# Remainders of plain weight blocks by a negated copy on ScalarE and an accumulating DMA, in place of a subtraction on VectorE

## The chip, the cores and the metric

The kernel runs on one core of one Trainium2 chip, as one launch. The metric is the device time of that launch in microseconds (us), the median of three runs. Beside it stands one profiled execution, whose trace gives the start and the duration of every instruction on TensorE (PE, its weight loads PEld), VectorE (DVE), ScalarE (ACT) and GpSimd (POOL), and the issue and landing of every DMA. SyncE (SP) only issues DMAs here.

## The reference

One inference step of a one-layer trunk on 640 tokens (512 of a prompt, 8 x 16 of running streams), model width 1024. The combined projection `z = x @ w_in` has 6656 columns, which are split into the inputs of three branches; then comes the output projection and a SwiGLU block, each with a LayerNorm.

```python
z = x @ w_in
xa, ya, glu, q, gates = jnp.split(z, COL_SPLITS, axis=-1)
xa_c = causal_depthwise_conv(xa_hist, conv_a_w, conv_a_b)          # width 4
h, h_last = rg_lru(xa_c, h_prev, ...)                              # gates by block products, then a scan
out_a = (h * jax.nn.gelu(ya)) @ proj_a
u = glu[..., :D_CONV] * jax.nn.sigmoid(glu[..., D_CONV:])
v = causal_depthwise_conv(u_hist, conv_b_w, conv_b_b)              # width 31
out_b = jax.nn.silu(layer_norm(v, ln_b_g, ln_b_b)) @ proj_b
out_c = mem_cross_attention(q, mem_k, mem_v) @ proj_c
g = jax.nn.sigmoid(gates + b_gate)
merged = g[:, :, 0] * out_a + g[:, :, 1] * out_b + g[:, :, 2] * out_c
x = layer_norm(DEEPNORM_ALPHA * x + merged @ w_out, ln1_g, ln1_b)
ffn = (jax.nn.silu(x @ w_ffn_gate) * (x @ w_ffn_up)) @ w_ffn_down
x = layer_norm(DEEPNORM_ALPHA * x + ffn, ln2_g, ln2_b)
```

All inputs and outputs are float32.

## The kernel before, in words

**Three products for one.** Each float32 factor is held as two parts in the type fp32r, which TensorE multiplies fast: `hi`, the rounded value, and `lo`, the remainder. A product is `hi·hi + hi·lo + lo·hi`. The activations stand as `xh` and `xl`, a weight block as `wh` and `wl`. For a weight block the raw float32 values come from memory into a tile `wr`; ScalarE copies them with rounding into `wh` (`prep_hi`, the call of `copy`), and VectorE subtracts, `wl = wr - wh` (`prep_lo`).

**Steps and loads.** The program is a list of `Step`s, run in order. A plain block is a step made by `x_step`: 128 columns of a weight against the 640 tokens in two halves `c` of 320, over eight rows of 128, so 48 matmuls (`fm`), in the order `hi·xh`, `hi·xl`, `lo·xh` for each row: the remainder is first needed by the fifth and sixth matmul of a block. One `Load` of 1 MB brings two blocks; there are two `wr` tiles, and a new load is issued by SP (`pump`, line 253) when both blocks of a tile have been used up (`take`, called in `prep_lo`).

**When a block is prepared.** At step i the loop at the end of `trunk` first calls `prep_hi` for the block of step i+2; then it issues the first matmuls of step i, then the eviction of step i-1 (`flush`), then pieces of the side work (`advance`), then `prep_lo` of the block of step i+2. `wh` and `wl` have three buffers each, so the copy for step i+2 waits for the last matmul of step i-1. Results stand in PSUM in the tiles `pu`, four of them, two to a step: step i+1 needs the two that step i-1 used, when their eviction is done.

**Side work.** The convolutions, the attention, the recurrence (`lru`) and the LayerNorms are generators ("streams"). `advance` takes pieces from them as long as a reckoned time of VectorE and ScalarE, kept by `price_vector` and `price_scalar`, is behind that of TensorE. Each engine runs its own instructions in the order in which they were written down. POOL issues the loads of the attention caches (line 997), of the recurrence's weights (line 1163) and a few stores, and runs some small operations.

**The blocks by name**, in the order of the steps: the GLU gates 0 and 1 and the GLU input 0 (one group of three, whose matmuls are mixed), GLU input 1 ("GA1"), four blocks of the query ("Q0" to "Q3"), GLU gates 2, 3 and inputs 2, 3; eight recurrence inputs ("XA0" to "XA7"); eight gates of branch 2 ("C2_0" to "C2_7"), eight blocks of `proj_c`; then gates of branch 1 in pairs ("C1_0" and "C1_1", ...), each pair followed by two blocks of `proj_b` of half the length ("pb0", "pb1", ...); eight recurrence gates ("YA0" to "YA7"); then products by another scheme (`seven`), `proj_a`, `w_out`; the first four blocks of the feed-forward (gate 0, gate 1 and up 0 in a group of three, and up 1, "UP1"), and the rest by `seven` and by tokens.

`x_step` is called 48 times. Six of the calls belong to the two groups of three.

## Time and profile before

| | |
|---|---|
| median of 3 runs | 1047.9 us (1047.83 to 1047.99) |
| profiled execution | 1048.17 us, its span 1046.4 us |
| granted TensorE clock | 0.998 |
| TensorE busy | 1034.9 us |
| VectorE busy | 801.9 us |
| ScalarE busy | 499.2 us |
| GpSimd busy | 83.8 us |
| DMA | 128.89 MB; the queue of POOL's DMAs 28.23 MB |

A share of the whole span is a mean over many stages. The questions for this change are asked of single places: when a block's parts are ready, when the first matmul needs them, and what stands in the same queue.

### The profile page before, as it was taken

How to read it: one execution, taken by the hardware profiler on the slowest of the kernel's cores; microseconds unless marked ns; L12 is line 12 of the kernel's file. 1: busy time of each engine (PE TensorE's matmuls, PEld its weight loads, DVE VectorE, ACT ScalarE, POOL GpSimd, SP SyncE). 2: the span in 40 equal slices, each digit the busy share in tenths (PEclk: the TensorE clock that was granted, in tenths of full speed). 3: DMA queues.
4: the chain of work that ended last, by engine and by line, in shares of the span. 5: the costliest groups of instructions: out<-in, count | busy, mean ns of one | idle time of the engine just before them, and what ended most of it. 6: DMA issues, size and time to landing. Idle time of an engine off the chain costs nothing.

```text
span 1046.4 us, 16741 instructions
## 1 busy us (share of the span) xinstructions
PE 1034.9 (99%) x6689; PEld 984.0 (94%) x6689; DVE 801.9 (77%) x1412; ACT 499.2 (48%) x894; POOL 83.8 (8%) x152
## 2 busy tenths in 40 slices
PE   9999999999999999999999999999999999999997
PEld 5899999999999999999998899999999999888886
DVE  5769988899657855999595578888888887576875
ACT  5733655254576449566232455444444334444350
POOL 0000404200000000000211210000000001000111
PEclk9999999999999999999999999999999999999999
DMA  9722216531121221212636222222222223733581
GB/s 346 256 96 82 89 42 228 205 105 56 41 101 61 102 81 47 81 62 79 256 149 220 102 101 79 84 81 81 82 81 87 101 96 106 312 125 122 181 281 40
DMA packets 29854, 128.89 MB, mean 123 GB/s; under 512 B 4016, under 2 KB 4848, under 8 KB 19920
## 3 DMA queue, kind: packets, MB, share of 16 engines
q1 hardware_dynamic: 21168, 99.59, 26.9%
q0 software_dynamic: 8608, 28.23, 7.4%
q8 instruction: 52, 0.85, 0.3%
q14 instruction: 26, 0.21, 0.1%
HBM read 115.31 MB, written 12.50 MB: 122 GB/s over the span
## 4 chain that ended last, share of the span: by engine, by line
PE 92%; DVE 3%; ACT 2%; DMA 2%; issue 1%; SPq 0%; DVEq 0%; POOL 0%; ACTq 0%
PE pu L64 82%; PE pv L64 10%; DVE s L64 1%; ACT s L64 1%; DVE wl L64 1%; DMA s<-in_w_mem_v 1%; DMA s<-in_w_mem_k 0%; DMA s<-in_x_prompt 0%; DVE xres L64 0%; ACT wh L64 0%; ACT xh L64 0%; DVE wh L64 0%; DVE st L64 0%; DVE xl L64 0%; ACT L64 0%
## 5 line engine op out<-in xcount | busy, mean ns | idle before, releaser
L64 PE MATMUL pu<-xh,wh 128*128 128x320 f32 x1040 | 243.0, 310 | 1.1 <-DVE wh L64 0.6
L64 PE MATMUL pu<-xh,wl 128*128 128x320 f32 x1040 | 241.2, 309 | 0.0
L64 ACT ACTIVATE wh<-wr 128x1024 fp32r<-128x1024 f32 (+1 forms) x149 | 135.0, 908 | 214.2 <-PE pu L64 125.2
L64 PE MATMUL pu<-xl,wh 128*128 128x320 f32 x888 | 213.5, 309 | 0.0
L64 DVE TENSOR_TENSOR s<-s,s 128x640 f32<-128x640 f32 (+5 forms) x206 | 144.8, 722 | 52.6 <-ACT s L64 50.0
L64 PE MATMUL pu<-s,wh 128*128 128x320 f32 x1064 | 184.6, 309 | 0.0
L64 PEld LDWEIGHTS pu<-xh,wh 128*128 128x128 f32 x1040 | 175.2, 188 | 3.2 <-ACT xh L64 1.0
L64 PEld LDWEIGHTS pu<-xh,wl 128*128 128x128 f32 x1040 | 175.7, 188 | 0.0
L64 DVE TENSOR_TENSOR wl<-wr,wh 128x1024 fp32r<-128x1024 f32 (+1 forms) x113 | 129.2, 1145 | 56.4 <-ACT wh L64 56.3
L64 PEld LDWEIGHTS pu<-s,wh 128*128 128x128 f32 x1064 | 163.2, 188 | 0.3 <-DVE wh L64 0.3
L64 PEld LDWEIGHTS pu<-xl,wh 128*128 128x128 f32 x888 | 151.9, 188 | 0.0
L64 PE MATMUL pu<-s,wl 128*128 128x320 f32 x808 | 146.9, 309 | 0.5 <-DVE s L64 0.5
L64 DVE TENSOR_TENSOR s<-s,pu 128x320 f32<-128x320 f32 x188 | 88.6, 485 | 64.1 <-PE pu L64 60.7
L64 ACT ACTIVATE s<-s 128x640 fp32r<-128x640 f32 (+4 forms) x148 | 90.0, 627 | 87.4 <-DVE s L64 76.3
L64 PEld LDWEIGHTS pu<-s,wl 128*128 128x128 f32 x808 | 125.5, 188 | 0.9 <-issue 0.9
L64 DVE SCALAR_TENSOR_TENSOR s<-s,pb,s 128x511 f32<-128x511 f32 (+14 forms) x240 | 112.1, 539 | 2.9 <-ACT s L64 2.9
L64 PE MATMUL pu<-wh,s 128*128 128x512 f32 x364 | 107.1, 383 | 0.1
L64 PEld LDWEIGHTS pu<-wh,s 128*128 128x128 f32 x364 | 66.8, 188 | 14.2 <-ACT wh L64 1.2
L64 ACT ACTIVATE s<-pu 128x320 f32<-128x320 f32 (+2 forms) x90 | 36.5, 439 | 66.6 <-PE pu L64 66.4
L64 PE MATMUL pu<-s,s 128*128 128x512 f32 (+1 forms) x236 | 61.7, 411 | 0.5 <-DMA s<-in_w_mem_k 0.5
L64 PE MATMUL pu<-wl,s 128*128 128x512 f32 x182 | 57.1, 381 | 0.0
L64 PEld LDWEIGHTS pu<-s,s 128*128 128x128 f32 x236 | 42.6, 188 | 14.8 <-issue 5.5
(124 smaller groups left out, 1123.0 us busy)
## 6 DMA issues: line engine op xcount, KB each, us to landing
wr<-in_w_in SPq DMA_DIRECT2D x26, 1024.0 KB, 4.8
wr<-in_w_ffn_down SPq DMA_DIRECT2D x19, 1024.0 KB, 4.9
wr<-in_w_ffn_gate SPq DMA_DIRECT2D x11, 1024.0 KB, 4.7
wr<-in_w_ffn_up SPq DMA_DIRECT2D x11, 1024.0 KB, 4.8
s<-in_cache_k POOLq DMA_DIRECT2D x16, 256.0 KB, 5.2
s<-in_cache_v POOLq DMA_DIRECT2D x16, 256.0 KB, 5.1
wr<-in_proj_a SPq DMA_DIRECT2D x4, 1024.0 KB, 7.7
wr<-in_w_out SPq DMA_DIRECT2D x4, 1024.0 KB, 4.9
```

Source lines behind the costliest of these rows:

```text
L64: return f(*a, **k)
```

## The change

`Step` gets an argument `dram`. Where it is given, `prep_hi` lets ScalarE write the block twice: rounded into `wh`, and with scale -1 into `wl`. Then POOL issues a DMA that takes the block from memory once more (512 KB) and adds it to what stands in `wl`; the weight minus its rounded value is left. `prep_lo` no longer subtracts for such a block. It still calls `take`, so the load that follows waits for the readers of `wr` that are left, which are ScalarE's. `x_step` gives `dram` where `group` is None.

```diff
-                     half=None, after=None):
+                     half=None, after=None, dram=None):
+            self.dram = dram
...
-            for h, _, x in self.todo:
+            for h, l, x in self.todo:
                 copy(h, x)
+                if self.dram is not None:
+                    A.activation(l, x, AF.Copy, scale=-1.0)
+            if self.dram is not None:
+                h, l, x = self.todo[0]
+                G.dma_start(l, self.dram(self.ld.ap()), accum_op=OP.add)
             self.w = (hi, lo)
...
-            for h, l, x in self.todo:
+            for h, l, x in self.todo if self.dram is None else ():
                 self.eng.tensor_tensor(l, x, f32(h), op=OP.subtract)
             self.todo = None
             self.ld.take()
...
-        s = Step(ld, lambda r: r[:, o // 128], [128, KD, 128], mm, lambda: evac([x[:, :HT] for x in s.p]))
+        s = Step(ld, lambda r: r[:, o // 128], [128, KD, 128], mm, lambda: evac([x[:, :HT] for x in s.p]),
+                 dram=(lambda w: w[:, o // 128]) if group is None else None)
```

## The prediction

> **What bounds the kernel now.** I read the page first, then the table of windows, then the groups, then the timeline at single places.

> ```profile
> span 1046.4 us, 16741 instructions
> PE 1034.9 (99%) x6689; PEld 984.0 (94%) x6689; DVE 801.9 (77%) x1412; ACT 499.2 (48%) x894; POOL 83.8 (8%) x152
> ...
> PE 92%; DVE 3%; ACT 2%; DMA 2%; issue 1%; SPq 0%; DVEq 0%; POOL 0%; ACTq 0%
> ```

> TensorE is busy for 99% of the span and is 92% of the chain that ended last. The windows say how much it ever waits (columns: stretch, length, then busy time of PE, PEld, DVE, ACT, POOL):

> ```profile
> 49.00:1038.00 989.00, 987.57 (x6466) 949.04 (x6466) 764.62 (x1333) 465.73 (x833) 78.50 (x138) 1.00 0.32 114
> 49.00:454.00 405.00, 405.00 (x2930) 401.43 (x2930) 319.64 (x596) 219.93 (x412) 37.03 (x68) 1.00 0.26 92
> 454.00:456.00 2.00, 1.29 (x7) 0.76 (x6) 2.00 (x5) 0.96 (x2) 0.00 (x0) 1.00 0.00 0
> 649.00:651.00 2.00, 1.76 (x12) 1.52 (x11) 1.69 (x4) 0.00 (x0) 0.00 (x0) 1.00 0.00 0
> ```

> Between 49 and 1038 us it stands still for 989.00 - 987.57 = 1.43 us, half of that (0.71) at 454 to 456, where VectorE is busy throughout, and 0.24 at 649. So relief of VectorE can give back 1.43 us at the very most. What counts is whether a new wait reaches TensorE.

> **The change, part by part.**

> ```profile
> L64 DVE TENSOR_TENSOR wl<-wr,wh 128x1024 fp32r<-128x1024 f32 x97 | 118.2, 1221 | 46.3 <-ACT wh L64 46.3
> L64 ACT ACTIVATE wh<-wr 128x1024 fp32r<-128x1024 f32 x97 | 102.5, 1060 | 186.1 <-PE pu L64 97.2 <-issue 46.2 <-PE pv L64 23.8
> wr<-in_w_in SPq DMA_DIRECT2D x26, 1024.0 KB, 4.8
> wr<-in_proj_b SPq DMA_DIRECT2D x4, 512.0 KB, 3.2
> ```

> Of the 48 calls of x_step 42 are outside the groups, so by the code 42 blocks change, not 48. *Removed:* 42 subtractions of 1.22 us, 51 us of VectorE. It hides under TensorE nearly everywhere, so I count no gain except at the 0.71 us stop, where nothing removed lies near (the last removed one is in YA7); I credit 0.4 us, half of it. *Added on ScalarE:* 42 copies of the same shape as wh, 1.06 us each, 45 us on an engine with 499 busy. *Added on POOL:* 42 DMAs of 512 KB.

> *The landing of the new DMA* is the unknown; no accumulating DMA is in the trace. A plain 512 KB takes 3.2 us, which is the lower bound. An addition has to fetch the old contents too, so 1 MB passes the engines; a plain 1 MB takes 4.8. POOL's own loads are slower than SP's: 256 KB on a quiet stretch took 3.1, nearly what SP needs for twice that, so I add 0.5 and take **5.3 us** when nothing else moves. Beside a load these rows stand:

> ```profile
> L1163 POOL DMA_DIRECT2D s<-in_lru_w x1: 536/536/536, 298.7 to 298.7; - x1
> DMA to landing us min/median/max: 3.1/3.1/3.1
> L253 SPq DMA_DIRECT2D wr<-in_w_in x1: 328/328/328, 182.1 to 182.1; - x1
> DMA to landing us min/median/max: 8.3/8.3/8.3
> L997 POOL DMA_DIRECT2D s<-in_cache_v x4: 536/536/545, 182.6 to 184.3; - x4
> DMA to landing us min/median/max: 6.6/7.4/7.6
> ```

> Four loads of POOL, together 1 MB, beside one 1 MB load of SP landed after 6.6 to 7.6 us. An accumulate that moves 1 MB beside a load is that case; I take **7.6**. For the upper bound I let the addition cost 3 us more in both cases (8.3 and 10.6: the load's row above shows that crowding alone can take 8.3 instead of 4.8).

> *How long the DMA may take* is read at each block: the start of wh, plus 2 x 1.06 us for the two copies, plus 0.1 for the semaphore, against the first matmul that reads wl. Most blocks have 9 to 16 us, for two whole blocks (14 us) lie between. The short ones follow a group of three or two half-length pb steps:

> ```profile
> 51.98 1.06 ACT L64 ACTIVATE wh<-wr 128x1024 fp32r<-128x1024 f32 x1 [2.25 <-PE pu L64]
> 54.32 0.33 SPq L253 DMA_DIRECT2D wr<-in_w_in  x1
> 59.41 0.45 PE L64 MATMUL pu<-xh,wl 128*128 128x320 f32 x2
> 312.21 1.06 ACT L64 ACTIVATE wh<-wr 128x1024 fp32r<-128x1024 f32 x1 [0.52 <-PE pu L64]
> 319.93 0.46 PE L64 MATMUL pu<-xh,wl 128*128 128x320 f32 x2
> 354.45 1.06 ACT L64 ACTIVATE wh<-wr 128x1024 fp32r<-128x1024 f32 x1
> 363.05 0.46 PE L64 MATMUL pu<-xh,wl 128*128 128x320 f32 x2
> 626.27 1.06 ACT L64 ACTIVATE wh<-wr 128x1024 fp32r<-128x1024 f32 x1 [3.68 <-PE pu L64]
> 632.09 0.33 SPq L253 DMA_DIRECT2D wr<-in_w_ffn_up  x1
> 633.69 0.46 PE L64 MATMUL pu<-xh,wl 128*128 128x320 f32 x2
> ```

> - GA1: issue at 51.98 + 2.12 + 0.1 = 54.2, needed at 59.41: 5.2 us. It is the second block of its tile, so take lets SP issue the next 1 MB load as soon as the negated copy is done, at the same moment (in the rows it goes out at 54.32, after the subtraction). 7.6 - 5.2 = **2.4 us** of waiting.
> - UP1: issue at 628.5, needed at 633.69: 5.2 us, and again the next load (632.09 in the rows, after a late subtraction) moves up to 628.4. **2.4 us.**
> - C1_2: issue at 314.4, needed at 319.93: 5.5 us, first block of its tile, no load beside it: 5.3 lands 0.2 before. C1_4 is alike. C1_6: 356.7 to 363.05, 6.4 us. Nothing, but if the cover is gone each us late costs a us.

> *ScalarE's queue.* Behind the negated copy stands the eviction of the step before, on which PSUM of the step after depends. It is 1.06 us later. Where a softmax or a table load has already held ScalarE up, that is not free:

> ```profile
> 211.31 0.94 ACT L64 ACTIVATE s<-pu,pa 128x320 f32<-128x320 f32 x2
> 212.55 0.46 PE L64 MATMUL pu<-xh,wh 128*128 128x320 f32 x2
> 314.58 0.94 ACT L64 ACTIVATE s<-pu,pa 128x320 f32<-128x320 f32 x2
> 315.82 0.75 PE L64 MATMUL pu<-s,wh 128*128 128x320 f32 x4
> 409.55 0.77 ACT L64 ACTIVATE s<-pu 128x320 f32<-128x320 f32 x2
> 410.86 0.46 PE L64 MATMUL pu<-xh,wh 128*128 128x320 f32 x2
> ```

> The second half's matmul comes 0.15 after the first. At 212: eviction ends 212.25 + 1.06 = 213.31 against 212.70, 0.6 late. At 315: 316.58 against 315.97, 0.6. At 410: 411.38 against 411.01, 0.4. Together **1.6 us**. The dispatcher's reckoned time of ScalarE grows by the copy too, so side work moves elsewhere; bounds 0 and twice that (3.2).

> *POOL's queue.* The DMA waits for ScalarE, and everything behind it on POOL waits with it. Today POOL runs far ahead of the program:

> ```profile
> 175.06 2.70 POOL L997 DMA_DIRECT2D s<-in_cache_k  x5 [4.28 <-PE pv L64]
> 194.52 1.86 PE pv L64 x32
> 203.62 1.86 PE pv L64 x32
> ```

> The key loads of heads 2 and 3 stand in the program after the scores of heads 0 and 1 (194.52), yet were issued by 177.8. Now they stand behind C2_1's accumulate, which goes out at about 189.9; eight issues end at 194.2. With SP's load and the accumulate's double traffic 4 MB are under way from 189.4. Two MB side by side took 8.3 us in the rows above; two more at 3.2 each (4.8 against 3.2 us for half a MB more) make 14.7: landed at 204.1, head 2's half 3.2 earlier. Needed are head 2's keys at 203.62 and head 3's half of 1.86 us later, at 204.5. Zero, but with 0.4 us to spare. The recurrence's weights come later as well, and ScalarE's rounding of them waits in queue some 4 us; the step's eviction stands before it, so zero too. SP's queue gains: loads go out earlier, but had time.

> **Sum:** 2.4 + 2.4 + 1.6 - 0.4 = 6.0 us. From the profiled execution's 1048.17 this gives 1054.2; the median stood 0.27 lower, so **1053.9**.

> [...]

> **Rivals.**

> *The DMA is hidden anyway* (chance 0.29). It lands like a plain copy: 3.2 to 3.7 quiet, and beside a load no later than the 5.2 us that GA1 and UP1 have, or SP's load loses the race. Then only the evictions count, 0 to 1.6, less 0.4: 1047.5 to 1049.1. For it: the DMA share in the window row from 49 to 454 is 0.26. Against: the load leaves at the very same moment.

> *The addition is slow* (0.18). At 8.3 and 10.6 us: GA1 and UP1 5.4 each, C1_2 and C1_4 2.8 each, C1_6 1.9, the keys of head 3 up to 2.6 (3 less the 0.4), evictions 1.6, less 0.4: 22.1 us, 1070.0. Over 14 us even ordinary blocks would wait and it would be 42 times the excess; I give that 0.03 of the 0.18. Nothing in the trace speaks for or against a rate of adding.

> *Faster* (0.03). VectorE's relief decides at 454 and 649, where its queue is what TensorE waits for: all 1.43 us come back, 1046.5. It decides only if every new DMA lands inside 5.2 us and evictions keep their margins; even then it is inside 0.2%, so more than that needs the start as well, and no changed block is prepared before 52 us.

> **How the numbers follow.** A measurement of this kernel tells about 0.2% (2.1 us) from no change. My case, waits of 2.1 to 12 us, has 0.50; hidden 0.29; slow 0.18; faster 0.03. So faster 0.03, same 0.29, slower 0.68. The range takes in the hidden case from 1047.2 and the slow one to 1070. The likeliest case's own range is 1050 to 1060.

> **What would show it.** VectorE's wl rows 97 down to 55; 42 ACT rows that write wl and 42 POOL DMAs into wl, landing 5 to 8 us. TensorE's waits at 59.4 and 633.7 released by a DMA into wl, about 2.4 us each, in place of nothing; waits on ACT near 212, 315 and 410; none in Q, XA or most of C2. Wrong if the DMA lands under 5 us beside a load, if it takes over 8 alone, or if POOL's cache loads arrive late and TensorE stops at the scores near 204.

## The result, and the profile after

The changed kernel takes 1084.2 us (median of 4 runs, 1083.1 to 1084.7) against 1047.95; the ratio is 1.0343, with an interval of 1.0331 to 1.0355. The forecast was 1053.9 with a range up to 1070: slower, as predicted, but by 36.2 us where 6.0 were.

The page of the changed kernel:

```profile
span 1083.0 us, 16839 instructions
PE 1045.8 (97%) x6689; PEld 992.1 (92%) x6689; DVE 755.0 (70%) x1370; ACT 539.0 (50%) x937; POOL 119.2 (11%) x194
...
L298 POOL DMA_DIRECT2D wl<-in_w_in x41 | 36.3, 886 | 330.4 <-ACT wl L64 278.0
...
wl<-in_w_in POOLq DMA_DIRECT2D x41, 512.0 KB, 7.8
```

The work moved as the diff says. VectorE has 42 instructions and 46.9 us less, ScalarE 39.8 us more, and POOL issues 41 accumulates from `w_in` and one from `w_ffn_up`. TensorE has the same 6689 matmuls, but its busy time is 10.9 us longer (1045.8 against 1034.9). The rest of the loss is idle time. The windows (stretch, length, busy time of PE, PEld, DVE, ACT, POOL, then the granted clock, the DMA share and GB/s), and after them the list of what TensorE waited for (total, times, longest):

```profile
49.00:1075.00 1026.00, 998.62 (x6472) 956.73 (x6471) 718.05 (x1292) 505.36 (x876) 114.55 (x180) 0.99 0.44 131
```

```profile
PE pu L64 <- DMA wl<-in_w_in: 11.4, 4, 3.9
PE pv L64 <- ACT s L64: 8.7, 1, 8.7
PE pv L64 <- DVE s L64: 3.0, 1, 3.0
PE pu L64 <- DMA wl<-in_w_ffn_up: 2.5, 1, 2.5
```

TensorE now stands still for 1026.00 - 998.62 = 27.4 us, where it was 1.4. So 26.0 us are stops and 10.9 us longer busy time; together 36.9, and the span grew by 36.6. The first and the fourth row are accumulates that land late. The second is one single stop of 8.7 us.

Most of the longer busy time follows the stops. Three stops (60 us, 236 us, 321 us), each with the stretch behind it:

```profile
59.40:62.70 3.30, 0.02 (x1) 0.00 (x0) 0.43 (x2) 1.53 (x3) 0.88 (x1) 0.84 1.02 176
62.70:71.70 9.00, 8.97 (x43) 8.97 (x44) 0.00 (x0) 0.00 (x0) 0.00 (x0) 0.68 0.76 211
...
236.20:244.90 8.70, 0.02 (x3) 0.01 (x3) 1.31 (x2) 2.42 (x6) 4.07 (x8) 0.67 1.03 325
244.90:251.90 7.00, 7.00 (x84) 6.39 (x85) 4.55 (x10) 3.92 (x7) 0.00 (x0) 0.68 0.43 158
320.80:324.70 3.90, 0.04 (x2) 0.03 (x1) 3.74 (x6) 3.83 (x6) 0.03 (x1) 0.97 0.94 216
324.70:328.50 3.80, 3.80 (x16) 3.80 (x17) 0.00 (x0) 0.31 (x1) 0.00 (x0) 0.58 1.02 287
```

TensorE is busy throughout behind each stop, but at 0.58 to 0.68 of the clock. Up to 1075 us the record of the clock has four spells at 0.5: from 61.6 for 6.8 us, from 225.5 for 3.4, from 239.1 for 10.2 and from 324.5 for 3.4, 23.9 us in all. The later part of a stop can lie in a spell, so TensorE works for only 16.9 of the 23.9 us; half of that, 8.4 us, is lost to the clock. The other 2.5 of the 10.9 us are something else: a run below with the negated copies alone has no such spell, and its TensorE is busy for 2.2 us longer too (1037.1). All the stops of the kernel after that are longer than 1 us:

| start, us | length | at | released by | halved clock behind it |
|---|---|---|---|---|
| 59.4 | 3.3 | GA1 | its accumulate (8.5 us to landing) | 6.8 |
| 222.3 | 3.0 | C2_2, sums of a LayerNorm | VectorE, side work | 3.4 |
| 236.2 | 8.7 | C2_3, attention values | ScalarE, which waited for the recurrence's weights | 10.2 |
| 320.8 | 3.9 | C1_0 | its accumulate, issued late | 3.4 |
| 354.7 | 2.0 | C1_3 | its accumulate | none |
| 428.6 | 2.3 | YA1 | its accumulate | none |
| 668.1 | 2.55 | UP1 | its accumulate (7.8 us) | none |

GA1 and UP1 were named in the prediction. The other five were not.

The 8.7 us stop is read on two queues. POOL and ScalarE in the kernel after (start, duration, what; in brackets the idle time before it and what ended it):

```profile
233.96 0.90 POOL L298 DMA_DIRECT2D wl<-in_w_in  x1 [10.85 <-ACT wl L64]
234.52 1.46 POOL L1170 DMA_DIRECT2D s<-in_lru_w  x2
```

```profile
232.61 1.04 ACT L64 ACTIVATE wl<-wr 128x1024 fp32r<-128x1024 f32 x1
242.48 1.25 ACT L64 ACTIVATE s<-s 128x512 fp32r<-128x512 f32 x2 [8.82 <-DMA s<-in_lru_w]
243.63 0.93 ACT L64 ACTIVATE s<-pu,pa 128x320 f32<-128x320 f32 x2
244.45 1.21 ACT L64 ACTIVATE s<-pv 128x256 f32<-128x256 f32 x4
```

and POOL in the kernel before:

```profile
207.53 1.06 POOL L1163 DMA_DIRECT2D s<-in_lru_w  x2
```

The two loads of the recurrence's weights stood behind nothing that waits and went out at 207.5. Now they stand behind C2_5's accumulate, which POOL may issue only when ScalarE has written the negated copy, and go out at 234.5. ScalarE's next instruction rounds these weights, so ScalarE stands still for 8.8 us, and behind it in its queue stand an eviction and the copies of the attention that TensorE needs.

### The profile page after: what moved, and what is told of

Same layout as the page of the kernel before. It is cut to its first block, busy times and chain, and to the rows that moved or that the text cites. A ratio compares the mean times of both kernels' runs of the same rounds, so it can differ in the third digit from the quotient of the medians.

```text
span 1083.0 us, 16839 instructions
## 1 busy us (share of the span) xinstructions
PE 1045.8 (97%) x6689; PEld 992.1 (92%) x6689; DVE 755.0 (70%) x1370; ACT 539.0 (50%) x937; POOL 119.2 (11%) x194
## 3 DMA queue, kind: packets, MB, share of 16 engines
q0 software_dynamic: 14656, 50.25, 18.3%
## 4 chain that ended last, share of the span: by engine, by line
PE 60%; issue 6%; DMA 3%; DVE 1%; ACT 0%; POOL 0%; DVEq 0%; POOLq 0%; ACTq 0%
PE pu L64 54%; PE pv L64 5%; DMA wl<-in_w_in 2%; DMA wl<-in_w_ffn_up 1%; DVE xres L64 0%; DVE s L64 0%; DVE wl L64 0%; ACT wh L64 0%; ACT wl L64 0%; POOL wl L298 0%; DVE xl L64 0%; DVEq L2012 0%; ACT xh L64 0%; DVE wh L64 0%; DVE st L64 0%
## 5 line engine op out<-in xcount | busy, mean ns | idle before, releaser
L64 PE MATMUL pu<-xh,wl 128*128 128x320 f32 x1040 | 244.0, 312 | 13.9 <-DMA wl<-in_w_in 11.4
L64 PE MATMUL pu<-xh,wh 128*128 128x320 f32 x1040 | 245.1, 313 | 0.6 <-ACT xh L64 0.5
L64 ACT ACTIVATE wh<-wr 128x1024 fp32r<-128x1024 f32 (+1 forms) x149 | 134.9, 908 | 221.7 <-PE pu L64 126.0
L64 PE MATMUL pu<-xl,wh 128*128 128x320 f32 x888 | 215.2, 311 | 0.0
L64 DVE TENSOR_TENSOR s<-s,s 128x640 f32<-128x640 f32 (+5 forms) x206 | 144.8, 723 | 83.8 <-ACT s L64 81.1
L64 PEld LDWEIGHTS pu<-xh,wl 128*128 128x128 f32 x1040 | 177.3, 190 | 15.6 <-DMA wl<-in_w_in 12.6
L64 PE MATMUL pu<-s,wh 128*128 128x320 f32 x1064 | 184.9, 309 | 1.1 <-DVE s L64 1.1
L64 PEld LDWEIGHTS pu<-xh,wh 128*128 128x128 f32 x1040 | 177.2, 190 | 2.6 <-issue 1.2
L64 DVE TENSOR_TENSOR s<-s,pu 128x320 f32<-128x320 f32 x188 | 88.7, 486 | 116.8 <-PE pu L64 113.5
L64 PEld LDWEIGHTS pu<-s,wh 128*128 128x128 f32 x1064 | 163.2, 188 | 1.9 <-DVE s L64 1.8
L64 PEld LDWEIGHTS pu<-xl,wh 128*128 128x128 f32 x888 | 153.7, 190 | 0.0
L64 PE MATMUL pu<-s,wl 128*128 128x320 f32 x808 | 146.9, 309 | 0.2 <-DVE s L64 0.2
L64 ACT ACTIVATE s<-s 128x640 fp32r<-128x640 f32 (+4 forms) x148 | 90.1, 628 | 98.4 <-DVE s L64 80.9
L64 PEld LDWEIGHTS pu<-s,wl 128*128 128x128 f32 x808 | 125.6, 188 | 0.7 <-issue 0.5
L64 DVE SCALAR_TENSOR_TENSOR s<-s,pb,s 128x511 f32<-128x511 f32 (+14 forms) x240 | 110.8, 535 | 4.6 <-ACT s L64 4.4
L64 PE MATMUL pu<-wh,s 128*128 128x512 f32 x364 | 107.1, 383 | 0.1
L64 DVE TENSOR_TENSOR wl<-wr,wh 128x1024 fp32r<-128x1024 f32 (+1 forms) x71 | 77.9, 1101 | 32.2 <-ACT wh L64 32.1
L64 PEld LDWEIGHTS pu<-wh,s 128*128 128x128 f32 x364 | 66.8, 188 | 13.9 <-ACT wh L64 0.8
L298 POOL DMA_DIRECT2D wl<-in_w_in x41 | 36.3, 886 | 330.4 <-ACT wl L64 278.0
L64 ACT ACTIVATE s<-pu 128x320 f32<-128x320 f32 (+2 forms) x90 | 36.6, 440 | 66.7 <-PE pu L64 66.5
L64 ACT ACTIVATE wl<-wr 128x1024 fp32r<-128x1024 f32 (+1 forms) x78 | 66.2, 849 | 0.0
L64 PE MATMUL pu<-s,s 128*128 128x512 f32 (+1 forms) x236 | 61.8, 413 | 0.0
## 6 DMA issues: line engine op xcount, KB each, us to landing
wr<-in_w_in SPq DMA_DIRECT2D x26, 1024.0 KB, 5.8
wl<-in_w_in POOLq DMA_DIRECT2D x41, 512.0 KB, 7.8
wr<-in_w_ffn_down SPq DMA_DIRECT2D x19, 1024.0 KB, 4.8
wr<-in_w_ffn_gate SPq DMA_DIRECT2D x11, 1024.0 KB, 4.8
wr<-in_w_ffn_up SPq DMA_DIRECT2D x11, 1024.0 KB, 4.8
wr<-in_proj_a SPq DMA_DIRECT2D x4, 1024.0 KB, 6.3
```

The lines of the kernel that those rows point to most:

```text
L64: return f(*a, **k)
L298: G.dma_start(l, self.dram(self.ld.ap()), accum_op=OP.add)
```

## The experiments

One ladder takes the loss apart. Each rung is one edit more, and each has a run of its own:

| kernel | us | rung |
|---|---|---|
| after | 1084.2 | |
| the order of before kept | 1068.3 | 15.9 |
| and 12 blocks with a short lead subtract again | 1059.2 | 9.1 |
| and the recurrence's weights are loaded earlier (some side work moves with them) | 1052.4 | 6.7 |
| before | 1048.0 | 4.5 |

**The order of before.** The dispatcher no longer charges VectorE for the 42 subtractions, and charges ScalarE for 42 copies; so it writes the pieces of the side work down at other places. Here both charges are as they were, and with them the order: apart from the copies into `wl` and the subtractions, the traces show TensorE, VectorE and ScalarE running the same sequence as before.

```diff
                 if self.dram is not None:
+                    at = A.time
                     A.activation(l, x, AF.Copy, scale=-1.0)
+                    A.time = at
...
-            for h, l, x in self.todo if self.dram is None else ():
-                self.eng.tensor_tensor(l, x, f32(h), op=OP.subtract)
+            for h, l, x in self.todo:
+                if self.dram is None:
+                    self.eng.tensor_tensor(l, x, f32(h), op=OP.subtract)
+                else:
+                    V.time += price_vector(V, "tensor_tensor", (l,), {})
```

> The changed kernel, but the reckoned times that place the side work are those of the kernel before (VectorE is still charged for the 42 subtractions, ScalarE is not charged for the 42 negated copies), so the instructions stand in the order of before. Theory A (three things add up: short leads, POOL's order, moved side work; and the halved clock after long stops): only the moved side work goes, that is the stop of 3.0 us at 222 and the late negated copy of C1_0 (3.9 us), with 3.4 us of halved clock: about 1076 us (1069 to 1080). Rival B (the moved side work is the root of it all): 1048 to 1056. Rival C (ScalarE's longer queue is the root): no change, 1082 to 1086.

Measured: 1068.3 us, ratio 1.0193 (1.0178 to 1.0208), just below the range of theory A and far above that of rival B: the moved side work is worth more than A held, and it is not the whole. What TensorE waits for:

```profile
PE pu L64 <- ACT s L64: 5.4, 2, 4.5
PE pu L64 <- DMA wl<-in_w_in: 3.5, 1, 3.5
PE pu L64 <- DMA wl<-in_w_ffn_up: 2.3, 1, 2.3
```

The stops at 222, in C1 and in YA1 are gone. GA1, UP1 and a stop of 4.5 us at 239 stay, each with a spell of 3.4 us behind it. So 15.9 us of the loss are the moved side work, the largest share.

**Which charge moves it.** As the changed kernel, but ScalarE is not charged for its copies (the first hunk above alone); VectorE stays uncharged.

> The changed kernel, but ScalarE's reckoned time is not charged for the negated copies; VectorE's is not charged for the subtractions either, as in the change. Together with the kernel that keeps both as before (1068.3) it tells which of the two reckoned times moves the side work. If VectorE's does: near the changed kernel, 1078 to 1088, with a stop where TensorE waits for VectorE near 222. If ScalarE's does: near 1068.

Measured: 1083.7 us, ratio 1.0346 (1.0315 to 1.0376), as slow as the kernel after. The charge of ScalarE, which the prediction had named, isn't needed for a loss of this size; the missing charge of VectorE is enough. The pieces don't come to stand quite where they do in the kernel after: the stop near 222 that was expected isn't in the profile, and stops on side work lie at 239, 247 and 338 us instead. The mirror image, VectorE alone charged, was not run. An example of a moved piece, the sums of a LayerNorm on TensorE, first in the kernel before, then after:

```profile
249.71 1.24 PE L64 MATMUL pv<-s,ones 128*128 128x512 f32 x4
```

```profile
225.34 2.34 PE L64 MATMUL pv<-s,ones 128*128 128x512 f32 x4 [3.01 <-DVE s L64]
```

The dispatcher holds VectorE to be free earlier and writes this piece down 24 us sooner, before VectorE has its input ready; TensorE starts nothing behind it and waits 3.0 us. With VectorE's charge alone missing the piece stands as early, at 222.0, but TensorE waits only 0.3 us for it.

**The recurrence's weights.** The edits of two runs differ in one thing. Both keep the old charges, and in both the 12 blocks that the timeline showed short of time (GA1, C1_0 to C1_7, YA0, YA1, UP1) subtract; 30 use the accumulate. `SHORT` holds the numbers of the blocks that subtract. In the second the first two loads of `lru_w` are written down three steps earlier, at the start of C2_0.

```diff
-                 dram=(lambda w: w[:, o // 128]) if group is None else None)
+                 dram=(lambda w: w[:, o // 128]) if group is None and len(plain) not in SHORT else None)
...
+        if i == first["pc"] - 8:
+            for z in range(2):
+                raws[0, z] = ri_load(0, z)
```

> The order of the instructions of before is kept, the 12 blocks with a short lead keep the subtraction, 30 blocks have the negated copy and the accumulate; the loads of the recurrence's weights stand where they stood, behind the accumulate of C2_5. It differs from the run at 1052.4 in these loads alone. Theory L (the loads behind a waiting accumulate hold ScalarE up, and TensorE with it): a stop of about 4.5 us near 239 with 1.7 us of halved clock, 1058.6 us (1057 to 1060). Rival (moving the loads only moved a wait from one place to another, so it is worth nothing): 1052 to 1053.5.

> Three repairs at once: order of the side work as before, subtraction kept in the 12 blocks with short leads, recurrence weights loaded three steps earlier; 30 blocks by DMA. Theory A: what is left is ScalarE's copies (about 2 to 3 us of the 4.1 that the copies alone cost) and some late key loads of the cache (1 us): 1050 to 1053. Rival D (the DMA's traffic itself slows everything): over 1058. Rival F, that side work or evictions find other places to be late: 1054 to 1060.

Measured: 1059.2 us, ratio 1.0104 (1.0087 to 1.0121), and 1052.4, ratio 1.0044 (1.0029 to 1.0059). ScalarE and TensorE's waits in the first:

```profile
237.22 1.22 ACT L65 ACTIVATE s<-s 128x512 fp32r<-128x512 f32 x2 [11.55 <-DMA s<-in_lru_w]
...
239.16 0.92 ACT L65 ACTIVATE s<-pu,pa 128x320 f32<-128x320 f32 x2
```

```profile
PE pu L65 <- ACT s L65: 5.7, 2, 4.8
PE pv L65 <- DMA s<-in_cache_k: 1.7, 1, 1.7
```

and ScalarE in the second:

```profile
231.40 1.04 ACT L65 ACTIVATE wl<-wr 128x1024 fp32r<-128x1024 f32 x1
232.34 1.14 ACT L65 ACTIVATE s<-s 128x512 fp32r<-128x512 f32 x2
```

Both came out inside their ranges. Against the kernel with the order alone, the first lacks the stops of GA1 and UP1 with their spells: 3.5 + 1.7 + 2.3 + 1.7 = 9.2 us, and 9.1 were measured. In the second the weights have landed by 208.4, the rounding follows a negated copy at once, and the stop of 4.8 us and the 1.7 us for its spell are gone.

The two differ in more than the loads, though: earlier loads also made the planner place side work elsewhere. In the second kernel the rounding stands one block later, and TensorE, VectorE and ScalarE run pieces between 232 and 330 us in another order; the sequence of before is kept only in the first. The wait for the weights goes all the same, for 208.4 lies ahead of both places of the rounding, and from 245 to 410 us neither profile has a stop over 0.6 us. What the moved pieces are worth was not measured by itself. By the medians the rung is 6.7 us; the two profiled executions lie 8.5 apart, for the first also stops for 1.7 us at 196, where a load of keys for attention head 1 lands late. The prediction did not look at this load; the keys of heads 2 and 3, to which it had left "0.4 us to spare", came in time there.

**The same two edits without their partners.** The 12 blocks subtract, with the charges of after; the loads earlier, charges of after; and loads earlier with the charges of before, all 42 blocks by DMA. Each of these edits moves some side work as well, so none of the three isolates its wait:

> The changed kernel with the subtraction on VectorE kept in the 12 plain blocks that have little time between preparation and use (GA1, the eight gates of branch 1, YA0, YA1, UP1); 30 blocks by DMA. Theory A: the waits for a DMA into wl go (3.3 + 3.9 + 2.0 + 2.3 + 2.6 = 14 us) and two of the four stretches of halved clock (5.1 us): about 1065 (1060 to 1069). Rival B: a gain only where the order moves by chance, over 1075. A rival D, that the DMA's extra traffic itself slows everything: the loss goes with the count, 30 of 42 blocks: 1074.

> The changed kernel with the two loads of the recurrence's weights (line 1170 there, POOL) written down three steps earlier, at the start of C2_0 instead of within C2_3. Theory A: the 8.7 us stop at 236 goes with its 5.1 us of halved clock: about 1070 (1068 to 1074). A rival E, that the stop is the late value loads of the cache (same POOL queue, issued after the accumulate as well): 1080 to 1086, the stop stays. Rival B: the stop shrinks only if the side work moves: 1080 or more.

> Order of the side work as before and the recurrence weights loaded three steps earlier, all 42 blocks by DMA. Theory A: against the kernel with the order alone (1068.3) the stop of 4.5 us at 239 and its 1.7 us of halved clock go: 1062 (1060 to 1064). If that stop is not due to those loads: 1067 to 1069.

Measured: 1070.8 (ratio 1.0218, 1.0202 to 1.0235), 1077.8 (1.0287, 1.0269 to 1.0305) and 1068.0 (1.0186, 1.0169 to 1.0203). All three lie above the ranges of their theories A. The first two match no rival either; the third has the time of its rival, but not its sign, for the stop at 239 is gone. In the first the stops of GA1, C1 and UP1 went, but another piece of side work, 468 us in, made TensorE wait 4.7 us. In the second the 8.7 us stop went, and ScalarE waited 5.5 us, until 356, for the second pair of the same loads, with 3.7 us of TensorE behind it. The third missed its 1062 by 6 us. In place of the stop at 239 stands C1_3:

```profile
341.06 0.56 PE L64 MATMUL pu<-xh,wl 128*128 128x320 f32 x2 [3.57 <-DMA wl<-in_w_in]
```

Its accumulate goes out at 332.55 and lands at 341.0, as in the run with the order kept alone (332.64 and 341.0). But there TensorE, held up before, reached the block only at 340.67, and here at 336.74. Here the copies ought to have come earlier too, and did not: the earlier loads moved a piece of the recurrence in front of them. ScalarE in this run,

```profile
327.74 1.69 ACT L64 ACTIVATE s<-s,lru 128x640 f32<-128x640 f32 x2
...
329.96 1.04 ACT L64 ACTIVATE wh<-wr 128x1024 fp32r<-128x1024 f32 x1
```

and with the order kept alone, where that piece stands behind:

```profile
330.04 1.06 ACT L64 ACTIVATE wh<-wr 128x1024 fp32r<-128x1024 f32 x1
...
333.36 1.70 ACT L64 ACTIVATE s<-s,lru 128x640 f32<-128x640 f32 x2
```

With its table load the piece holds ScalarE from 326.44 to 329.96, 3.5 us, as long as the stop. So this miss is moved side work once more. The spell behind GA1's stop was 6.8 us long in the profiled execution instead of 3.4, most of the rest of the balance. An edit that repairs one wait can shift the plan and make another; that is why the ladder's rungs hold only in their order.

**The accumulate by itself.** The order of before, and only GA1 and UP1 by DMA (`SHORT` holds the other 40):

> The order of before is kept and only GA1 and UP1 have the negated copy and the accumulate; the other 40 blocks subtract. Theory S (each of the two lands late by itself, beside SP's load, and TensorE pays the stop and then a spell of halved clock): 3.5 + 1.7 and 2.3 + 1.7 us, 1057.1 us (1056 to 1058.5). Rival of the prediction's size (2.4 us each, no clock): 1052.8. Rival C (they land late because of the other 40 accumulates): under 1051.

Measured: 1054.9 us, ratio 1.0063 (1.0048 to 1.0078), between the first two expectations.

```profile
PE pu L65 <- DMA wl<-in_w_ffn_up: 2.9, 1, 2.9
PE pu L65 <- DMA wl<-in_w_in: 2.8, 1, 2.8
```

GA1's accumulate takes 8.0 us to land. Each is late by itself; no other accumulate is needed. The stops are a little over the 2.4 us predicted; one of them (GA1) has a spell of 3.4 us behind it, the other none. 2.8 + 1.7 + 2.9 = 7.4, and 6.7 were measured.

**Adding against copying.** The order kept, all 42, but the DMA overwrites instead of adding, so this kernel leaves out the remainder:

```diff
-                G.dma_start(l, self.dram(self.ld.ap()), accum_op=OP.add)
+                G.dma_start(l, self.dram(self.ld.ap()))
```

> Order of the side work as before; the DMA into wl is a plain copy instead of an accumulating one (it overwrites the negated weight, so the remainder is not computed; everything else, the wait for ScalarE too, stays). It measures what the addition itself costs: landing about 3.7 us quiet and 6.3 beside a load, against 5.2 and 7.9. Theory A: the stops at GA1 and UP1 shrink by 1.6 us each to 1.9 and 0.7 and lose their halved clock: about 1061 to 1064. If the addition is free: 1067 to 1069 and the same landings.

Measured: 1055.2 us, ratio 1.0070 (1.0055 to 1.0085), 13.1 us less than with the addition and below both expectations. GA1's DMA, beside a load, in the copying kernel and in the kernel after:

```profile
L300 POOL DMA_DIRECT2D wl<-in_w_in x1: 740/740/740, 53.7 to 53.7; - x1
DMA to landing us min/median/max: 5.7/5.7/5.7
```

```profile
L298 POOL DMA_DIRECT2D wl<-in_w_in x1: 1067/1067/1067, 54.2 to 54.2; - x1
DMA to landing us min/median/max: 8.5/8.5/8.5
```

C1_6's DMA, alone, takes 3.2 us as a copy and 5.4 in the kernel after. So the addition costs 2.2 us alone and 2.8 beside a load; against the kernel with the order kept, which differs in the addition only, it is 2.0 (5.2) and 3.0 (8.7). POOL needs 0.33 us more to issue it (0.864 against 0.538). With a copy GA1 and UP1 wait 0.4 us each instead of 3.5 and 2.3; the stop of 4.5 us behind the recurrence's weights, which wait in the same queue, shrinks to 1.9; and no stop brings a spell any more, where there were three of 1.7 us each. Together that is 3.1 + 1.9 + 2.6 + 5.1 = 12.7 of the 13.1 us.

**The negated copies alone.** 42 copies on ScalarE, then VectorE subtracts as before; no DMA, order kept.

> Only ScalarE's part of the change: the 42 negated copies are written into wl, then VectorE subtracts as before; no DMA on POOL, order of the side work as before. Theory A: the copy alone delays evictions by 1.06 us where they are tight, 0 to 3 us in all: 1048 to 1051. Rival C (ScalarE's longer queue is the root): over 1065. Rival B: 1048 to 1050, like A.

Measured: 1052.2 us, ratio 1.0040 (1.0026 to 1.0054), 4.1 more than the kernel before, which took 1048.1 beside it, and just above the expected 1051. Matched matmul by matmul against before, the three places of the prediction lose 0.6 (212 us), 0.6 (315) and 1.2 (410) us; the rest falls at 418 (0.5) and between 643 and 649 (0.8) and in steps too small to place. The ladder's last rung, 4.5 us with 30 copies and 30 accumulates, is about this size, so accumulates that have time to land cost little at most. ScalarE at 410, the place of the three that was mis-sized most:

```profile
410.10 1.04 ACT L64 ACTIVATE wl<-wr 128x1024 fp32r<-128x1024 f32 x1
411.17 1.28 ACT L64 ACT_TABLE_LOAD   x1
412.46 0.77 ACT L64 ACTIVATE s<-pu 128x320 f32<-128x320 f32 x2
```

The eviction starts at 412.46, 2.9 us later than the 409.55 of before, where the kernel as a whole is 1.0 us later: ScalarE's queue carries more than one copy's delay here.

**A stop without a DMA.** The kernel before, in which ScalarE repeats the rounding of three blocks, so that an eviction and TensorE come late:

```diff
             for h, _, x in self.todo:
                 copy(h, x)
+                at = A.time
+                for _ in range(self.again):
+                    copy(h, x)
+                A.time = at
```

> The kernel before, no accumulate; behind the rounding of three blocks ScalarE repeats the same copy, 8 times in the step of Q1 (73 us), 12 times in that of Q3 (87 us) and 8 times in that of XA4 (162 us), so that the eviction behind it and TensorE with it come late: by the slack in the rows of before, stops of about 3.3, 6.8 and 1.5 us, at places with no DMA for TensorE to wait for. Theory K (a stop of TensorE by itself brings the halved clock, in units of 3.41 us): one or two units after the first, two or three after the second, none after the third, 3 to 5 units in all, each 1.7 us: 11.6 + 5 to 8.5, 1064.6 to 1068.1 us. Rival D (the halved clock comes with the accumulating DMA and not with the stop): no spell at 0.5, 1059.6 us.

Measured: 1067.4 us, ratio 1.0184 (1.0169 to 1.0199). The three stops, each with the stretch behind it:

```profile
79.60:83.10 3.50, 0.04 (x2) 0.04 (x1) 0.58 (x2) 3.44 (x6) 0.00 (x0) 0.86 0.00 0
83.10:92.20 9.10, 9.10 (x43) 8.99 (x44) 9.10 (x19) 1.31 (x3) 0.00 (x0) 0.68 0.33 117
100.10:107.90 7.80, 0.06 (x2) 0.02 (x1) 0.57 (x2) 7.61 (x10) 0.00 (x0) 0.66 0.00 0
107.90:115.90 8.00, 8.00 (x41) 7.88 (x42) 8.00 (x17) 1.93 (x4) 0.00 (x0) 0.69 0.28 97
186.80:188.80 2.00, 0.02 (x1) 0.00 (x0) 0.00 (x0) 1.97 (x4) 0.52 (x1) 1.00 0.90 297
188.80:192.00 3.20, 3.19 (x20) 3.05 (x21) 1.18 (x4) 3.20 (x12) 0.00 (x0) 1.00 0.95 374
```

The stops of 3.5 and 7.7 us bring the halved clock (6.8 and 10.2 us of it), the one of 2.0 none, and the DMA share is 0.00 during the first two. Five units of 3.4 us are inside the three to five of theory K. The stop does it, not the transfer.

## Why the prediction was wrong, by its steps

*TensorE is the bound, and VectorE's relief gives nothing.* Right as far as the runs show: VectorE has 46.9 us less to do, and no run shows a gain from it. The credit of 0.4 us shows nowhere.

*The landing, 5.3 alone and 7.6 beside a load.* Nearly right: 5.4 alone and 7.8 to 8.5 beside one load; up to 9.9 (C1_1) where more was under way. The doubled bytes were the author's estimate; the traces count 512 KB for an accumulate as for a copy: POOL's queue holds 50.25 MB with either and 28.23 before. They show it in time instead: this queue's packets take 18.4% of the 16 engines' span with the addition (order kept), 13.4% with the copy and 7.4% before; over 42 DMAs the differences are 2.8 us of all 16 engines for an accumulate and 1.5 for a copy.

*GA1 and UP1, 2.4 us each.* The mechanism and the issue times were right (54.16 against 54.2); the stops are 3.3 and 2.55. GA1's landing at 8.5 instead of 7.6 is the difference.

*C1_2, C1_4 and C1_6, nothing.* Right: none of them stops TensorE. C1_0 and C1_3, which do, are late because moved pieces of side work stand before their copies on ScalarE; with the order kept they don't stop, and C1_3 stops again where the earlier loads had moved a piece in front of it.

*Evictions behind the copy, 1.6 us.* The places were right, the size was not: they lose 2.4 us, two places that were not named another 1.3, and all 42 copies together 4.1, more than the upper bound of 3.2.

*POOL's queue, "so zero too".* **This step failed.** Its premise, "the step's eviction stands before it", is not what the rows of before show. There the rounding stands between a copy into `wh` and the eviction behind that copy:

```profile
221.11 1.05 ACT L64 ACTIVATE wh<-wr 128x1024 fp32r<-128x1024 f32 x1
222.05 1.14 ACT L64 ACTIVATE s<-s 128x512 fp32r<-128x512 f32 x2
...
223.91 0.93 ACT L64 ACTIVATE s<-pu,pa 128x320 f32<-128x320 f32 x2
```

So when the rounding waits, this eviction is late, and in the kernel after also the attention's copies. Its "some 4 us" of waiting was 8.8 to 11.9 us in the runs. It cost 6.7 us, by the two runs whose edits differ in these loads; the side work that moved with them is in that number.

*The dispatcher's reckoned time, "bounds 0 and twice that (3.2)".* **This step failed most:** 15.9 us. It looked at the charge that was added, ScalarE's, and not at the one that fell away. The removed instruction was also a number in the planner, and 42 of them shift pieces that are placed by that number; the run without either of the two charges lost as much as the kernel after.

*The clock, not in the sum at all.* Every wait was priced at its own length. **This term was missing.** The halved clock behind the stops took 8.4 us, 23% of the loss. The rungs of the ladder hold their share of it. The longest wait in its sum was 2.4 us; GA1's was 3.3, with 6.8 us of halved clock behind it.

The range's upper end came from a slow addition, 8.3 us alone and 10.6 beside a load. It was not that slow, and the 1084.2 lie beyond that end by two terms held to be near zero and one that was missing. It is not free either: in the order of before a plain copy in its place takes 13.1 us less.

What stays open: which of the moved pieces cost what (only their sum is measured), how the 6.7 us divide between the loads and the pieces that moved with them, the 0.8 us at 643 to 649 and the longer busy time of TensorE in the run with the copies alone, and why the addition costs more beside a load.

## What to carry to other kernels

Where a program is laid out by reckoned engine times, moving work to another engine edits the plan as well as the work: first change the work with the old charges kept, and only then the charges. A DMA that must wait for an engine turns a queue that ran far ahead into one that follows it (here two loads went out at 234.5 us instead of 207.5); list every transfer behind it, and what stands behind each one's reader. And price a stop of a nearly full TensorE at its length plus the halved clock that may follow: in these runs 1.7 us for each 3.41 us of it in which TensorE works.

## What the runs showed of the hardware

```profile
638.40:641.40 3.00, 0.09 (x2) 0.04 (x1) 3.00 (x7) 1.66 (x3) 0.00 (x0) 1.00 0.66 131
641.40:648.00 6.60, 6.60 (x45) 6.60 (x46) 5.59 (x9) 3.26 (x6) 0.00 (x0) 1.00 0.01 2
```

A unit already at half clock was followed by another one at every idle share from 0.14 up (the lowest were 0.14, 0.27 and 0.32), while with 0.10 or less the clock came back.
